# Two-layer retention and convolution trunk: early function table, longer warm-up, later rotary steps, one more staged weight unit

## The chip, the cores and the metric

The kernel runs on one core of one Trainium2 chip. The metric is the device time of one execution in microseconds (us). Before the change it is 840.92 us, the median of 3 runs (840.57 to 841.09).

## The reference, cut to what matters

```python
def reference(x, mem, positions, ...):          # x (1,512,1024), mem (1,256,1024), f32
    mem_k, mem_v = split(rmsnorm(mem, mem_norm_g) @ w_mem_kv)
    for i in range(2):
        h = rmsnorm(x, norm_pre_g[i])
        if i == 0: branch, xq, gate = retention_branch(h @ ret_w_in[0], positions)   # rotary q, k
        else:      branch, xq, gate = conv_branch(h @ conv_w_in[0], ...)             # 31 taps
        y = concatenate([branch, memory_attention(xq, mem_k, mem_v)]) * silu(gate)
        x = x + rmsnorm(y @ w_out, norm_post_g[i])
    return x
```

All is f32. The rotary embedding multiplies pairs of q and k by the cosine and sine of position times frequency.

## The kernel before, in words

Every engine runs its instructions in the order in which the program writes them; nothing is reordered afterwards. The program is written as projections of 16 chunks of matrix products, and `weave` puts other steps ("sides") behind a given chunk: `(5, x_rstd)` means that `x_rstd` is written behind chunk 5. A chunk's own loads and conversions are written when the chunk is, ahead of its products.

**Weights.** Each weight matrix is cut into units of 256 rows by 512 columns, used one after the other: units 0 to 7 for the memory's keys and values, 8 to 55 for the input projection of layer 0, 56 to 71 for its output projection, from 72 on for layer 1. Each product of f32 matrices is done as three products of rounded parts (`split3`, lines 302 to 304): high times high, high times low, low times high. So a unit is loaded by SP's queue into `wraw` (line 172, three buffers), cast by ScalarE to its high half `whi` (line 192), and the rest is computed as the low half `wlo`, on VectorE for some units (line 196), on POOL (GpSimd) for the others in two parts (line 199). There are five buffers each for the halves. `next_unit` hands out the halves of the next unit and converts some units ahead (`sent["ahead"]`: three in layer 0, one in the first projection of layer 1).

**Staged units.** For the units in `PRE` (even numbers, 76 to 110) the split is done during layer 0: `split_ahead` loads half a unit, casts it (line 228), subtracts on POOL (line 229) and stores both parts in a DRAM buffer `ahead` (line 219). One such step runs every 6 chunks (`ahead_hook`) from the second x projection on. When the unit is due, `conv_units` issues two loads on SP's queue instead (lines 182 and 183).

**The head.** ScalarE's queue loads `gcols` (norm weights, line 445) and `ident` (line 451). SP's queue loads `mem_t` in four parts, with units 0 to 2 between them. TensorE does 10 products of a block of ones with itself (line 461, two instructions each). ScalarE then scales `mem_t` to its high part (`split_c`, line 468), VectorE computes the low part (line 472). The projection of the memory's keys follows (16 chunks of 6 products of 256 columns, units 0 to 3, four chunks each), then that of its values.

**The first x projection** (`proj_halves`, 8 chunks of 12 products, units 8 to 11) gives values `v`. Its four results stay in their accumulators until the scale of the norm of x is known. `x_rstd` (behind chunk 5) sums the squares with small products (line 495), copies the sums on VectorE (line 497) and takes the power on POOL (lines 382 and 385); then ScalarE evacuates the four accumulators to `vb` (line 855). The next projection, xq (units 12 to 15), needs the same four accumulators. The diagonals of the scale (line 390) are built behind chunk 7.

**Rotary tables.** `rope_tables` is a generator of 25 steps: step 1 issues two DMAs of the positions, steps 2 to 21 are VectorE work on 128x256 tiles (range reduction), step 22 two sines on ScalarE (lines 825 and 826), the rest VectorE. `steps(n)` writes the next n of them.

**The start of layer 1.** The last phase of layer 0's output projection finishes token blocks 0 to 3 in turn; `post` updates a block with two VectorE instructions (line 732), `fin0` stores it to DRAM on SP's queue (line 1046), `sq` and `scale` (lines 1055 and 1060) norm it, and TensorE transposes it (line 406). Layer 1's first projection is `proj_halves` in its other form: chunks 0 to 15 do the first two token blocks with units 72 to 75, four chunks each, while blocks 2 and 3 are still on their way. Its sides are: 0 a transposition, 2 `post` of block 3 with its store, 4 the transposition of block 2, 5 and 7 the norm of block 3, 9 its transposition:

```python
weave(proj_halves(hT, evac_ug(0)), fill=0.95, sides=
      [(0, lambda: x1_T(3)), (2, post3), (4, x1_T2), (5, lambda: sq(3)), (7, lambda: scale(3)), (9, x1_T3)])
```

Unit 73 is converted in chunk 0, 74 in chunk 4 and 75 in chunk 8, 74 with its low half on POOL.

Of the kernel before, what the change touches and what calls it, by code (L numbers as in the profile page):

```python
# [13 lines left out]
AF = mybir.ActivationFunctionType  # L14
# [5 lines left out]
P = 128  # L20
# [16 lines left out]
GAMMA_LOG = np.log1p(-np.exp2(-5.0 - np.arange(NH, dtype=np.float64)))  # L37
CHUNK_DECAY = [float(np.exp(P * g)) for g in GAMMA_LOG]

WARM = 10  # L40
RATE = (1.6, 2.1, 1.9, 1.9, 1.7, 2.0, 1.7, 1.9, 2.1, 1.9)
XA = {0: (0, 7, 12), 1: (4, 13, 20), 2: (10, 17, 27), 3: (14, 22, 30)}
OFFLOAD = (0, 0.4, 0.8, 0.8, 0.8, 0.8, 0.8, 0.9, 0.8, 0.4, 0.5)
LN = (7, 32, 34, 36, 39)
LATE = 123
PRE = range(76, 112, 2)
MAGIC = 12582912.0
TWO_PI = 2.0 * math.pi

# [43 lines left out]
def trunk(ctx, tc, x, x_t, mem_t, pos, g_cols, w_mem, post_g, w0, w1, dw_w, dw_b,  # L93
          ln_g, ln_b, c_mask, c_xi, c_zeta, c_inv, c_eye, out):
    nc = tc.nc
# [9 lines left out]
    def nm(s):  # L105
        uid[0] += 1
        return f"{s}_{uid[0]}"

    def mm_ps():
        return ps.tile([P, 512], F32, tag="mm", bufs=4, name=nm("mm"))  # L110
# [7 lines left out]
    def big(dt, shape):  # L118
        return gp.tile(shape, dt, tag="big", bufs=8, name=nm("big"))
# [4 lines left out]
    def tiny(shape):  # L124
        return gp.tile(shape, F32, tag="tiny", bufs=32, name=nm("tiny"))
# [4 lines left out]
    nhalf = gp.tile([P, 8], F32, name="nhalf")  # L130
# [32 lines left out]
    def send(upto):  # L163

        for i in range(sent["dma"], min(upto, sent["conv"] + 3, nu)):
            sent["dma"] = i + 1
            if i in PRE:
                continue
# [5 lines left out]
    def conv_units(upto):  # L174
        for i in range(sent["conv"], min(upto, nu)):
# [4 lines left out]
            sent["conv"] = i + 1  # L180
            if i in PRE:
                nc.sync.dma_start(out=hi.bitcast(F32), in_=ahead[i][:, :, 1])
# [20 lines left out]

    ahead = {i: dp.tile([P, 2, 2, G], F32, name=f"ahead{i}") for i in PRE}

    def split_ahead(pool):

        todo = [(i, k) for i in PRE for k in range(2)]
        stage = {}

        def load(n):
            if n < len(todo):
                i, k = todo[n]
                stage[n] = pool.tile([P, 2, G], F32, tag="stage", bufs=3, name=nm("stage"))
                nc.sync.dma_start(out=stage[n][:, 0], in_=units[i][:, k * G:(k + 1) * G])

        def store(n):
            i, k = todo[n]
            nc.sync.dma_start(out=ahead[i][:, k], in_=stage.pop(n))

        load(0)
        yield
        for n in range(len(todo)):
            if n:
                store(n - 1)
            load(n + 1)
            st = stage[n]
            nc.scalar.copy(out=st[:, 1].bitcast(F32R), in_=st[:, 0])  # L228
            nc.gpsimd.tensor_tensor(out=st[:, 0], in0=st[:, 0], in1=st[:, 1], op=ALU.subtract)  # L229
            yield  # L230
        store(len(todo) - 1)
# [45 lines left out]
    def weave(chunks, sides=(), fill=0.0):  # L277
        phase[0] += bool(fill)
        at = {}
        for pos_, fn, *cost in sides:  # L280
            at.setdefault(pos_, []).append((fn, *cost, 0.0))
        due = more = 0.0
        for i, c in enumerate(chunks):
            c()
            due += fill
            for fn, cost, *_ in at.pop(i, ()):
                fn()
                due += fill * cost
            for hook in hooks:
                hook()  # L290
            while due >= 1 and (behind or filler and filler[0][2] in (None, *gls)):
                due -= filler[0][0] if filler else 1
                step()
            due = min(due, 2.0)
            more = min(more + OFFLOAD[phase[0]], 2.0) if fill else 0.0
            while more >= 1 and offload and offload[0]():
                more -= 1
        assert not at, at
# [7 lines left out]
    def proj(hT, tok_major, evac, n=S):  # L306

        cnt = n // P if tok_major else 4
        acc, unit = [], []

        def chunk(u, a):
            if not acc:
                acc.extend(mm_ps() for _ in range(cnt))
            if a == 0:
                unit[:] = next_unit()
            hi, lo = unit
            for k in range(2):
                kt = 2 * u + k
                hs = hT(kt)
                if tok_major:  # L320
                    lhs = tuple(t[:, a * P:(a + 1) * P] for t in hs)
                    split3(acc[a], lhs, (hi[:, k, :], lo[:, k, :]), kt == 0, kt == 7)
                else:
                    lhs = tuple(w[:, k, a * P:(a + 1) * P] for w in (hi, lo))
                    split3(acc[a][:, :n], lhs, hs, kt == 0, kt == 7)
            if u == 3:
                evac(a, acc[a])

        return [lambda u=u, a=a: chunk(u, a) for u in range(4) for a in range(cnt)]
# [112 lines left out]


    mt = big(F32, [P, KD, M])
    nc.scalar.dma_start(out=gcols, in_=g_cols.rearrange("p (a k) -> p a k", a=3))
    for c in range(4):
        nc.sync.dma_start(out=mt[:, 2 * c:2 * c + 2], in_=mem_t[:, c * G:(c + 1) * G]
# [11 lines left out]
    warm = mm_ps()  # L459
    for i in range(WARM):  # L460
        nc.tensor.matmul(warm[:, :P], ones, ones, start=True, stop=True)
# [3 lines left out]
    def split_c(src, kp, gcol, dst):  # L465

        for kt in (2 * kp, 2 * kp + 1):
            nc.scalar.activation(out=dst(kt)[0], in_=src[:, kt], func=AF.Copy,
                                 scale=gcol[:, kt:kt + 1])
        for kt in (2 * kp, 2 * kp + 1):  # L470
            hi, lo = dst(kt)
            nc.vector.scalar_tensor_tensor(out=lo, in0=src[:, kt], scalar=gcol[:, kt:kt + 1],
                                           in1=hi.bitcast(F32), op0=ALU.mult, op1=ALU.subtract)
# [3 lines left out]
    def squares(key, xt):  # L477

        sq = red[key] = [w4([P, KD // 2, 256]) for _ in range(2)]
        for i in range(2):  # L480
            nc.scalar.activation(out=sq[i], in_=xt[:, 4 * i:4 * i + 4], func=AF.Square)
        nc.gpsimd.tensor_tensor(out=sq[0], in0=sq[0], in1=sq[1], op=ALU.add)

    def reduced(key):
        sq = red[key]
        nc.vector.tensor_reduce(out=sq[1][:, 0], in_=sq[0].rearrange("p k s -> p s k"),
                                axis=AX.X, op=ALU.add)
        red[key] = sq[1][:, 0]
# [40 lines left out]
    xS = lambda half, kp: lambda: split_c(xp[half], kp, gcols[:, 1], hdst(half))  # L529
# [93 lines left out]
    def evac_copy(dst):  # L623
        return lambda a, acc: nc.scalar.copy(out=dst[:, a, :], in_=acc)
# [135 lines left out]
    with tc.tile_pool(name="l0", bufs=1) as lp:  # L760
# [84 lines left out]
        def steps(n):  # L845
            return lambda: [next(rope_steps, None) for _ in range(n)]
# [31 lines left out]
        def evac_gx(a, acc):  # L878
# [3 lines left out]
        sent["ahead"] = 3  # L882
        weave(proj_halves(hT, lambda t, acc: evac_vb(0)(t, acc) if "c" in rx else
                          late_v.append((t, acc)), True),
              [(0, steps(1))] + [(kp, xS(1, kp)) for kp in range(4)]
              + [(1, lambda: squares(1, xp[1])), (1, lambda: reduced(0)), (2, lambda: reduced(1)),
                 (5, x_rstd), (5, mem_diags), (7, x_diags)] + [(c, steps(2)) for c in range(4, 8)])
        pace["steps"] = split_ahead(lp)
        hooks.append(ahead_hook)
        weave(proj(hT, False, evac_copy(xq)), [(0, mem_spread), (1, x_spread)]  # L890
              + [(c, steps(2)) for c in range(16)])
        gx = big(F32, [P, XH, S])
        weave(proj(hT, False, evac_gx))
        yx = [big(F32R, [P, XH, S]) for _ in range(2)]
# [556 lines left out]
```

## Time and profile before

| | |
|---|---|
| median of 3 runs | 840.92 us (840.57 to 841.09) |
| the profiled execution | 841.23 us |
| its span, first to last instruction | 839.4 us |
| mean granted TensorE clock | 0.983 |
| TensorE busy | 805.0 us (96%) |
| VectorE busy | 507.5 us (60%) |
| ScalarE busy | 359.6 us (43%) |
| POOL busy | 437.0 us (52%) |

Times in the rows are us from the start of the span. PE is TensorE, DVE VectorE, ACT ScalarE, POOL GpSimd, SP the engine whose queue issues most DMAs; a q behind an engine's name is its queue. L302 is line 302. A busy TensorE is not TensorE at its peak, since its products overlap.

### The profile page before, as it was taken

What the parts mean: (1) busy time and instruction counts of PE and PEld (TensorE: products, weight loads), DVE (VectorE), ACT (ScalarE), POOL (GpSimd) and SP (SyncE); (2) the same over time, 40 slices, a digit from 0 to 9 for tenths busy, and PEclk for the clock granted to TensorE, in tenths of its full rate; (3) what the DMA queues carried; (4) which work ended last, traced back from release to release, by engine and by line L of the source; (5) the groups of instructions that cost most, each with busy time, mean ns of one, the idle gap of its engine ahead of it and who ended that gap; (6) DMA issues with size and microseconds to landing.
All of it is one profiled execution on the core that took longest, in us unless ns stands there. A gap on an engine that the chain in (4) does not pass through costs nothing.

```text
span 839.4 us, 10668 instructions
## 1 busy us (share of the span) xinstructions
PE 805.0 (96%) x3904; PEld 675.2 (80%) x3904; DVE 507.5 (60%) x794; ACT 359.6 (43%) x599; POOL 437.0 (52%) x390
## 2 busy tenths in 40 slices
PE   8999999999999999999999999999997995799997
PEld 8878888888888888888888988888876874388886
DVE  5898112143664641442437489999987999656423
ACT  6844366522212143433426234634676741166311
POOL 1145554467767766212233329969960993259202
PEclk9999999999999999999999999999998998799999
DMA  7623644364344445657743444444432212122712
GB/s 274 252 96 126 214 151 132 112 220 138 124 152 163 150 127 176 219 180 250 255 149 122 177 155 148 153 135 130 145 119 75 76 58 93 46 82 75 251 51 100
DMA packets 43171, 122.74 MB, mean 146 GB/s; under 512 B 4976, under 2 KB 6640, under 8 KB 42864
## 3 DMA queue, kind: packets, MB, share of 16 engines
q1 hardware_dynamic: 42688, 121.86, 42.6%
q8 instruction: 30, 0.49, 0.2%
q10 hardware_dynamic: 432, 0.21, 0.1%
q14 instruction: 21, 0.17, 0.1%
HBM read 98.99 MB, written 23.07 MB: 145 GB/s over the span
## 4 chain that ended last, share of the span: by engine, by line
PE 78%; DVE 15%; ACT 4%; issue 2%; POOL 1%; DMA 0%; POOLq 0%; DVEq 0%; ACTq 0%
PE mm L304 22%; PE mm L302 22%; PE mm L303 22%; DVE acc L1138 8%; DVE cy L1210 1%; PE tp L592 1%; PE acc L975 1%; PE tp L550 1%; PE tp L956 1%; PE acc L977 1%; PE acc L302 1%; PE acc L303 1%; PE acc L304 1%; PE tp L933 1%; ACT w L563 1%
## 5 line engine op out<-in xcount | busy, mean ns | idle before, releaser
L199 POOL TENSOR_TENSOR wlo<-wraw,whi 128x512 fp32r<-128x512 f32 x148 | 193.0, 1329 | 154.7 <-ACT whi L192 151.5
L302 PE MATMUL mm<-big,whi 128*128 128x512 f32 (+1 forms) x608 | 236.4, 389 | 4.6 <-ACT whi L188 1.9
L304 PE MATMUL mm<-big,wlo 128*128 128x512 f32 (+1 forms) x608 | 228.0, 375 | 0.2 <-DVE wlo L189 0.2
L303 PE MATMUL mm<-big,whi 128*128 128x512 f32 (+1 forms) x608 | 227.5, 374 | 0.0
L1138 DVE SCALAR_TENSOR_TENSOR acc<-gl,taps,acc 128x512 f32<-128x512 f32 x278 | 186.3, 748 | 0.4
L304 PE MATMUL mm<-whi,big 128*128 128x512 f32 (+1 forms) x432 | 166.9, 386 | 0.0
L302 PE MATMUL mm<-whi,big 128*128 128x512 f32 (+1 forms) x408 | 162.0, 397 | 0.0
L303 PE MATMUL mm<-wlo,big 128*128 128x512 f32 (+1 forms) x408 | 157.7, 387 | 0.2 <-DVE wlo L196 0.2
L192 ACT CAST whi<-wraw 128x1024 fp32r<-128x1024 f32 x115 | 119.3, 1047 | 39.5 <-PE mm L304 18.8
L302 PEld LDWEIGHTS mm<-big,whi 128*128 128x128 f32 x608 | 115.6, 190 | 24.9 <-ACT whi L188 2.2
L304 PEld LDWEIGHTS mm<-big,wlo 128*128 128x128 f32 x608 | 115.3, 190 | 21.3 <-DVE wlo L189 0.6
L303 PEld LDWEIGHTS mm<-big,whi 128*128 128x128 f32 x608 | 115.6, 190 | 19.3 <-issue 1.0
L229 POOL TENSOR_TENSOR stage<-stage 128x512 f32<-128x512 f32 x36 | 49.2, 1367 | 92.2 <-ACT stage L228 92.2
L1123 POOL TENSOR_TENSOR part<-part,pr 128x512 f32<-128x512 f32 x70 | 90.8, 1336 | 9.0 <-ACT pr L1122 9.0
L304 PEld LDWEIGHTS mm<-whi,big 128*128 128x128 f32 x432 | 81.1, 188 | 16.9
L303 PEld LDWEIGHTS mm<-wlo,big 128*128 128x128 f32 x408 | 76.8, 188 | 15.2 <-DVE wlo L196 0.7
L302 PEld LDWEIGHTS mm<-whi,big 128*128 128x128 f32 x408 | 76.7, 188 | 14.4
L196 DVE TENSOR_TENSOR wlo<-wraw,whi 128x1024 fp32r<-128x1024 f32 x41 | 56.4, 1388 | 43.4 <-ACT whi L192 43.3
L1122 ACT ACTIVATE pr<-gl,taps 128x512 f32<-128x512 f32 x70 | 47.6, 717 | 7.0 <-POOL part L1123 5.8
L228 ACT CAST stage<-stage 128x512 fp32r<-128x512 f32 x36 | 22.3, 620 | 48.3 <-DMA stage<-in_w 30.0
L948 ACT ACTIVATE kz<-tp,zeta 128x384 f32<-128x384 f32 x8 | 4.7, 584 | 78.1 <-PE tp L946 78.1
L1096 ACT ACTIVATE gl<-mm 128x512 f32<-128x512 f32 x12 | 7.2, 600 | 48.6 <-PE mm L304 48.6
(216 smaller groups left out, 895.5 us busy)
## 6 DMA issues: line engine op xcount, KB each, us to landing
wraw<-in_w SPq DMA_DIRECT2D x108, 512.0 KB, 4.1
ahead<-stage SPq DMA_DIRECT2D x36, 512.0 KB, 5.2
stage<-in_w SPq DMA_DIRECT2D x36, 256.0 KB, 5.2
whi<-ahead SPq DMA_DIRECT2D x18, 512.0 KB, 4.2
wlo<-ahead SPq DMA_DIRECT2D x18, 512.0 KB, 6.3
wraw<-in_w_mem SPq DMA_DIRECT2D x7, 512.0 KB, 4.8
big<-in_x_t SPq DMA_DIRECT2D x2, 1024.0 KB, 5.7
o<-in_x SPq DMA_DIRECT2D x1, 2048.0 KB, 9.0
```

The source lines that it names most:

```text
L192: nc.scalar.copy(out=hi, in_=raw)
L196: nc.vector.tensor_tensor(out=lo, in0=raw, in1=hi.bitcast(F32), op=ALU.subtract)
L199: nc.gpsimd.tensor_tensor(out=lo[:, k], in0=raw[:, k], in1=hi[:, k].bitcast(F32), op=ALU.subtract)
L228: nc.scalar.copy(out=st[:, 1].bitcast(F32R), in_=st[:, 0])
L229: nc.gpsimd.tensor_tensor(out=st[:, 0], in0=st[:, 0], in1=st[:, 1], op=ALU.subtract)
L302: nc.tensor.matmul(dst, lh, rh, start=start, stop=False)
L303: nc.tensor.matmul(dst, lh, rl, start=False, stop=False)
L304: nc.tensor.matmul(dst, ll, rh, start=False, stop=stop)
L550: nc.tensor.matmul(sc[:, j * M:(j + 1) * M], xq[:, h, t * P:(t + 1) * P], mkT[:, h, :], start=True, stop=True)
L1122: nc.scalar.activation(out=pr, in_=gl[:, k:k + S], func=AF.Copy, scale=tap)
L1123: nc.gpsimd.tensor_tensor(out=parts[ct], in0=parts[ct], in1=pr, op=ALU.add)
L1138: nc.vector.scalar_tensor_tensor(out=o, in0=gl[:, k:k + S], scalar=tap, in1=ac, op0=ALU.mult, op1=ALU.add)
```

## The change

Four edits. `WARM` goes from 10 to 13 products. `PRE` starts at 74 instead of 76, so that unit 74 is staged too (38 steps of half a unit instead of 36). A small activation on a constant (8 columns, filled by a memset at the start) is written ahead of the DMA of `gcols` on ScalarE's queue; the compiler puts the load of the function table ahead of the first activation. The rotary steps are written later: step 1 behind chunk 3 of the first x projection instead of chunk 0, two steps behind chunk 7 instead of two behind each of chunks 4 to 7, and then three behind each chunk of xq instead of two.

```diff
-WARM = 10
+WARM = 13
...
-PRE = range(76, 112, 2)
+PRE = range(74, 112, 2)
...
     mt = big(F32, [P, KD, M])
+    first = tiny([P, 8])
+    nc.scalar.activation(out=first, in_=nhalf, func=AF.Copy, scale=nhalf[:, 0:1])
     nc.scalar.dma_start(out=gcols, in_=g_cols.rearrange("p (a k) -> p a k", a=3))
...
-              [(0, steps(1))] + [(kp, xS(1, kp)) for kp in range(4)]
+              [(3, steps(1))] + [(kp, xS(1, kp)) for kp in range(4)]
               + [(1, lambda: squares(1, xp[1])), (1, lambda: reduced(0)), (2, lambda: reduced(1)),
-                 (5, x_rstd), (5, mem_diags), (7, x_diags)] + [(c, steps(2)) for c in range(4, 8)])
+                 (5, x_rstd), (5, mem_diags), (7, x_diags), (7, steps(2))])
...
         weave(proj(hT, False, evac_copy(xq)), [(0, mem_spread), (1, x_spread)]
-              + [(c, steps(2)) for c in range(16)])
+              + [(c, steps(3)) for c in range(16)])
```

## Rows read from the trace of the kernel before

**Rows 1.** The page: the chain that ended last, shares of the span by engine.

```profile
PE 78%; DVE 15%; ACT 4%; issue 2%; POOL 1%; DMA 0%; POOLq 0%; DVEq 0%; ACTq 0%
```

**Rows 2.** TensorE's waits, whole span: total us, times, longest us.

```profile
PE tp L406 <- DVE w L1060: 1.3, 1, 1.3
```

**Rows 3.** Timeline of ScalarE, head: start, us, what, count, idle before and its releaser.

```profile
4.75 1.28 ACT L468 ACT_TABLE_LOAD   x1 [4.75 <-DMA big<-in_mem_t]
6.04 0.91 ACT L468 ACTIVATE big<-big,gcols 128x256 fp32r<-128x256 f32 x2
...
11.53 0.91 ACT L468 ACTIVATE big<-big,gcols 128x256 fp32r<-128x256 f32 x2 [0.75 <-DMA big<-in_mem_t]
```

**Rows 4.** Timeline of TensorE, head: the warm-up.

```profile
1.01 4.63 PE L461 MATMUL mm<-ones 128*128 128x128 f32 x20 [1.01 <-POOL ones L140]
```

**Rows 5.** Windows, head: length, busy by engine, granted clock, DMA share, GB/s.

```profile
6.00:9.00 3.00, 1.27 (x6) 0.88 (x7) 2.40 (x5) 2.85 (x8) 0.00 (x0) 1.00 0.99 384
9.00:12.00 3.00, 3.00 (x17) 3.00 (x18) 2.56 (x5) 2.25 (x5) 0.00 (x0) 0.57 0.89 318
12.00:15.00 3.00, 3.00 (x24) 3.00 (x24) 2.50 (x5) 3.00 (x5) 0.00 (x0) 0.86 0.55 194
```

**Rows 6.** Waits of SP's queue, 0 to 7 us.

```profile
SPq L172 <- DMA gcols<-in_g_cols: 1.4, 1, 1.4
```

**Rows 7.** Timeline of VectorE, head: the low halves of units 2 and 3.

```profile
13.41 2.36 DVE L196 TENSOR_TENSOR wlo<-wraw,whi 128x1024 fp32r<-128x1024 f32 x2 [0.45 <-ACT whi L192]
```

**Rows 8.** Chain of waits, head: the first product of chunk 8 (start, us).

```profile
15.74 0.12 PE mm L302
```

**Rows 9.** Timeline of ScalarE: the first evacuation of the memory's values.

```profile
31.65 0.69 ACT L517 ACTIVATE mv<-mm,tiny 128x512 f32<-128x512 f32 x1 [0.82 <-PE mm L304]
```

**Rows 10.** Timeline of VectorE ahead of the norm's scale.

```profile
50.33 0.28 DVE L789 CAST q<-posi 128x256 f32<-128x256 int32 x1
...
54.72 0.15 DVE L497 COPY tiny<-tp 128x4 f32<-128x4 f32 x1
```

**Rows 11.** Timeline of POOL there.

```profile
50.92 2.59 POOL L199 TENSOR_TENSOR wlo<-wraw,whi 128x512 fp32r<-128x512 f32 x2 [6.22 <-ACT whi L192]
54.96 0.19 POOL L382 TENSOR_SCALAR tiny<-tiny 128x4 f32<-128x4 f32 x1 [1.45 <-DVE tiny L497]
55.24 1.25 POOL L385 TENSOR_TENSOR tiny<-tiny,nhalf 128x4 f32<-128x4 f32 x1
```

**Rows 12.** Timeline of TensorE there.

```profile
55.77 0.39 PE L304 MATMUL mm<-whi,big 128*128 128x512 f32 x1
57.26 0.50 PE L302 MATMUL mm<-big,whi 128*128 128x512 f32 x1 [1.11 <-ACT vb L855]
```

**Rows 13.** Timeline of ScalarE: the first evacuation of xq.

```profile
76.64 0.59 ACT L624 COPY big<-mm 128x512 f32<-128x512 f32 x1 [1.14 <-PE mm L304]
```

**Rows 14.** Timelines of VectorE and POOL at the start of layer 1.

```profile
431.43 0.75 DVE L732 SCALAR_TENSOR_TENSOR o<-o,tiny 128x512 f32<-128x512 f32 x1 [0.38 <-POOL tiny L377]
...
451.29 1.61 DVE L732 SCALAR_TENSOR_TENSOR o<-o,tiny 128x512 f32<-128x512 f32 x1
452.83 1.77 DVE L732 SCALAR_TENSOR_TENSOR o<-ra,tiny,o 128x512 f32<-128x512 f32 x1
...
451.08 2.97 POOL L199 TENSOR_TENSOR wlo<-wraw,whi 128x512 fp32r<-128x512 f32 x2 [2.29 <-ACT whi L192]
```

**Rows 15.** Timeline of SP's queue there: the store of the last token block.

```profile
454.63 0.32 SPq L1046 DMA_DIRECT2D x1d<-o  x1
```

**Rows 16.** Issue to landing of the 18 loads of line 182, then of 183.

```profile
DMA to landing us min/median/max: 4.1/4.2/7.7
...
DMA to landing us min/median/max: 4.9/6.3/8.4
```

**Rows 17.** Timeline of TensorE, layer 1: unit 74's first low product, and chunk 10.

```profile
454.59 0.28 PE L304 MATMUL mm<-big,wlo 128*128 128x256 f32 x1
...
458.12 0.37 PE L302 MATMUL mm<-big,whi 128*128 128x256 f32 x1
```

## The prediction

> **What bounds the kernel now.** I read the chain of waits first: TensorE holds 78% of it and VectorE 15% [rows 1], and the VectorE part lies late in layer 1. So up to there a microsecond counts only if TensorE stands still in it or runs at the lower clock. Then I read TensorE's waits, its timeline around each wait, and last the engine that was waited for. Three places matter here.
>
> At the head, the products at line 461 end at 5.64 and the first real product starts at 7.5. In 6 to 9 us TensorE is busy 1.27 of 3.00, and the granted clock then stands at 0.57 and 0.86 in the next two stretches [rows 4, 5]: together (0.43 + 0.14) × 3 / 0.5 = 3.4 us at 1.2 instead of 2.4 GHz.
>
> At 55 us, the last product of the first x projection starts at 55.77 and the next one only at 57.26; at a step of 0.23 us, 1.26 us are lost. It waits for the first evacuation of `vb`, that one for POOL's power at 55.24 to 56.49, and that for VectorE's copy at 54.72 [rows 10 to 12]. Ahead of the copy VectorE ran rotary steps from 50.33 on.
>
> At the start of layer 1, TensorE waits 1.3 us at line 406 for the scale of the last token block [rows 2].
>
> **The function table.** The load takes 1.28 us and starts when the first quarter of `mem_t` has landed; the first activation follows at 6.04 [rows 3]. With the load done early, that activation waits for its data alone: mem_t by 4.7, and `gcols`, which landed at about 4.9 (a load of the third weight unit waited 1.4 us for just that landing [rows 6], since loads share completion counters). Now `gcols` is issued behind the table load and the small activation. How far that delays it the trace doesn't show, since no DMA stands behind a table load in it. Bounds: 0.1 us, if the queue passes the DMA on while the engine still loads; 1.28 + 0.46, if it holds it (half of the pair at 6.04, 0.91 us, is more than 8 columns can take [rows 3]). I take 0.1, as nothing in the DMA needs the engine. The first activation then starts at about 5.1 instead of 6.04; at the other end at about 6.7, and the third unit's load may then slip by the same 1.7 us.
>
> The Trainium skill ("Perfetto Trace Analysis", section "DVE / Act Engine Instruction") says that the sequencer is free again once it has pushed an activation into the wait queue, so the DMA would not wait for the load. By it the activation starts at 5.1, by a holding queue at 6.7; both give the same end below within 0.8 us.
>
> For what follows is set by data: the fourth quarter of mem_t lands at 11.53, ScalarE stands for it 0.75 us [rows 3], and only then casts units 2 and 3. So unit 2's low half stays ready at 14.6 (13.41 + half of 2.36 [rows 7]) however early the table is. TensorE used it first in the third product of chunk 8, 15.74 + 0.24 = 15.98 [rows 8]. So there are 1.4 us to gain at most, and TensorE can take them, because unit 1 is ready earlier still and three more warm products (six instructions of 4.63/20 = 0.23 us [rows 4]) run to about 7.0 and leave almost no idle time ahead of the first real one. Even a second fall of the clock would only use up time before 14.6. Further on, ScalarE caps it: it idles 0.82 us before the evacuation at 31.65 [rows 9], and its casts of units 10 and 11 stand behind that. Value **0.8 us gained**; bounds 0 and 1.4.
>
> **Rotary tables behind the scale.** Steps 2 to 9 leave the four chunks before the norm's scale; two come after the diagonals, the rest three a chunk. VectorE has unit 13's low half (1.2 us) left ahead of its copy, POOL unit 14's low halves, 2.59 us from 50.92 to 53.51 [rows 11]. So POOL is what comes last: it starts the scale at 53.55 instead of 54.96, and the first evacuation ends 1.4 us earlier, at about 55.8 against TensorE's 56.0. **1.26 us gained**, the whole gap, bounds 0 and 1.3; it holds if TensorE is 0.8 earlier, since POOL's unit 14 waits for TensorE to free a buffer. The positions' two DMAs move from chunk 0 to chunk 3, past no other load on SP's queue. The moved VectorE work, about 4 us, ends later: the two sines and the casts behind them come about 1 us later while TensorE is 2 us earlier. ScalarE has 1.14 us idle ahead of the next evacuation [rows 13] and the four accumulators are needed again only from 3.2 us later, so it costs nothing; were the tables over 3 us later, the excess would be lost.
>
> **One more staged unit.** Unit 74 is the third of layer 1's first projection, used from chunk 8 on. Its split moves into layer 0 (two more casts, two more subtractions, four more DMAs, in the last two paces of 6 chunks before the layer's end; they lie beside products, and the first scales needed there have over 2 us of slack): nothing. In layer 1 its cast and its two POOL subtractions go. Those, 2.97 us from 451.08, lie over VectorE's two updates of the last token block, which took 1.61 and 1.77 [rows 14]; without them I take 0.75 each, what the first of block 0 took [rows 14], and the scale comes 1.7 us earlier. That alone would remove the whole 1.3 us wait.
>
> But its halves now come by two loads on SP's queue, and they are issued in chunk 4, behind the store of the last token block (side 2), which waits for these very updates. The store went out at 454.63 [rows 15]; it now goes at about 452.85. Behind it the high half goes at 453.25 and the low half at 453.95 (issues of 0.32 and about 0.7). Landings of 18 such loads: 4.1 to 7.7 us for the high half, 4.9 to 8.4 for the low one, medians 4.2 and 6.3 [rows 16]. So the high half is there at 457.4, the low one between 458.8 and 462.3; I take 459.8, under the median sum of 460.2 because the queues are empty then. TensorE wants the low half at 454.59 [rows 17] (all in the time of before; the 2 us gained shift both sides alike).
>
> From that product to chunk 10 are 4 products and one chunk of 6 at 0.12 us a product [rows 8], and 8 transposes, 0.85 us: 0.48 + 0.72 + 0.85 = 2.05. Chunk 10 started at 458.12, wait included [rows 17]; now at 459.8 + 2.05 = 461.9. **3.8 us lost**, bounds 2.7 and 6.2. TensorE also does next to nothing from 454.4 to 459.8, less than in the stretch before the clock fell at the head [rows 5]. I expect the same fall: 3.4 us at half speed, **1.7 us lost**; bounds 0 and 3.4.
>
> The Trainium skill ("SBUF — State Buffer", section "SBUF: two separate sides") says that VectorE and GpSimd hold a shared port pair for whole instructions. The stretched updates agree (1.61 against 0.75), and by this rule alone the third edit is a gain of 1.3 us, which is the first rival.
>
> **The sum** on the profiled execution, 841.23 us (span 839.4 and 1.8 around it): − 0.8 − 1.26 + 3.8 + 1.7 = + 3.4, so 844.7; that execution lies 0.3 above the median of 840.92, so **844.4 us**. Layer 1 passes a delay on, because its VectorE work starts with the first projection's result.
>
> **Rivals.**
> - *The staged unit is in time*: its halves land before 454.6, TensorE loses its 1.3 us wait instead, and the time is 840.92 − 2.1 − 1.3 = 837.5. For it: the stretched updates are real, and other staged units are waited for nowhere. Against: those are issued far ahead, this one four chunks ahead. It needs issues at least 6 us ahead of use, that is ahead of the store. The change ends faster than before if the low half is used before about 458.1 and the clock stays up: 3.5 us over the 454.59.
> - *The stall without the fall of the clock*: 842.7. For it: a wait of 1.3 us here left no mark; against, the stall is four times as long.
> - *The head doesn't do what it says* (the DMA of gcols held, the third unit late, or the gap at 56 filled by something else): + 0.8 to + 2.1 on the forecast, 845.2 to 846.5.
> - *The edits at the head do what they say and more*: up to 1.4 there, 843.8; inside the range.
>
> **How the numbers follow.** Forecast 0.53, stall without the clock 0.15, unit in time 0.14, head without gain 0.13, else 0.05. What differs by under 0.2% (1.7 us) can't be told from no change. Faster by more than that: the unit in time, and a little else, 0.16. Within: half of the second rival and the forecast's low end (both halves landing at their fastest), 0.15. Slower: 0.69. The range leaves out the unit in time (0.14) and little above: 840.5 to 847.0; the forecast's own is 842.5 to 846.
>
> **What would show it.** Head: table load before 2.2 us, first activation near 5.1, no clock under 1.00 before 13 us or none that costs. At 55 us: the copy at line 497 some 4 us earlier against its neighbours, no wait of line 302 for `vb`. Layer 1: the updates at line 732 at 0.75 each, no wait of line 406, and in its place a TensorE wait of 4 to 6 us at line 302 and 304 for DMA of `whi` and `wlo` from `ahead`, with a clock near 0.5 behind it. Without that last wait the prediction is wrong.

## The result and the profile after

The changed kernel takes 846.05 us (median of 6 runs, 845.09 to 847.79), the kernel before 840.95 us beside it (6 runs, 839.74 to 841.47). The ratio is 1.0066 (95% interval 1.0053 to 1.0079), so 4.5 to 6.6 us slower. The profiled execution took 845.96 us, its span is 844.2.

The chain that ended last, from the page, and TensorE's waits of the whole span (total us, times, longest us). These answer to [rows 1, 2].

```profile
PE 76%; DVE 14%; ACT 4%; DMA 3%; issue 1%; POOL 1%; SPq 0%; POOLq 0%; DVEq 0%; ACTq 0%
```

```profile
PE mm L302 <- DMA whi<-ahead: 4.1, 1, 4.1
PE mm L303 <- DVE wlo L196: 1.9, 1, 1.9
PE mm L304 <- DMA wlo<-ahead: 0.6, 1, 0.6
```

DMA has come into the chain with 3%; it had 0%. The waits of 1.3 us at line 406 and of 1.1 us for `vb` are gone, and in their place stand 4.1 and 0.6 us for the two halves of a staged unit, and 1.9 us for a low half that VectorE makes.

I set the start of each TensorE instruction against that of the same instruction before (after minus before, us). The line numbers are 2 higher behind line 445.

```
at        25    41    50    57   451   472   632   639   718   724   span
change  -0.9  +0.9  +0.9  -0.4  -0.4  +5.4  +5.4  +4.5  +5.1  +4.2  +4.8
```

Three places hold most of it: 1.8 us lost between 25 and 41, 1.3 won at 57, 5.8 lost at 454 to 466.

**Head.** ScalarE's timeline, then three stretches (busy us of TensorE, its weight loads, VectorE, ScalarE and POOL; granted clock, DMA share, GB/s), as [rows 3, 5].

```profile
0.72 1.28 ACT L446 ACT_TABLE_LOAD   x1 [0.72 <-PEq L1444]
0.86 0.39 ACTq L447 DMA_DIRECT2D gcols<-in_g_cols  x1
...
5.02 0.91 ACT L470 ACTIVATE big<-big,gcols 128x256 fp32r<-128x256 f32 x2 [2.71 <-DMA gcols<-in_g_cols]
```

```profile
6.00:9.00 3.00, 2.78 (x20) 2.32 (x19) 2.53 (x6) 2.56 (x5) 0.00 (x0) 1.00 1.04 415
9.00:12.00 3.00, 2.88 (x24) 2.68 (x23) 2.53 (x5) 2.26 (x6) 0.00 (x0) 1.00 0.87 337
12.00:15.00 3.00, 2.73 (x23) 2.53 (x22) 2.55 (x3) 3.00 (x4) 0.00 (x0) 1.00 0.35 135
```

The table load runs from 0.72, `gcols` is issued at 0.86, inside it, and the first activation starts at 5.02. The clock doesn't fall.

**The scale of the norm.** VectorE's copy and the first evacuation of `vb`, as [rows 10, 12].

```profile
52.15 0.15 DVE L499 COPY tiny<-tp 128x4 f32<-128x4 f32 x1
```

```profile
56.07 2.42 ACT L857 ACTIVATE vb<-mm,tiny 128x512 f32<-128x512 f32 x4 [4.31 <-POOL tiny L385]
```

**Start of layer 1.** SP's queue, VectorE's two updates, TensorE's products of unit 74, and the stretches there, as [rows 14, 15, 17].

```profile
452.35 0.32 SPq L1048 DMA_DIRECT2D x1d<-o  x1
452.76 0.59 SPq L182 DMA_DIRECT2D whi<-ahead  x1
453.40 0.62 SPq L183 DMA_DIRECT2D wlo<-ahead  x1
```

```profile
450.92 0.74 DVE L734 SCALAR_TENSOR_TENSOR o<-o,tiny 128x512 f32<-128x512 f32 x1
451.58 0.75 DVE L734 SCALAR_TENSOR_TENSOR o<-ra,tiny,o 128x512 f32<-128x512 f32 x1
```

```profile
458.26 0.58 PE L302 MATMUL mm<-big,whi 128*128 128x256 f32 x1 [4.11 <-DMA whi<-ahead]
...
459.60 0.58 PE L304 MATMUL mm<-big,wlo 128*128 128x256 f32 x1 [0.55 <-DMA wlo<-ahead]
```

```profile
454.00:457.00 3.00, 0.15 (x2) 0.00 (x0) 1.89 (x2) 0.01 (x1) 0.28 (x3) 0.95 0.91 234
457.00:460.00 3.00, 1.19 (x4) 0.90 (x5) 0.00 (x0) 0.00 (x0) 0.00 (x0) 0.50 1.02 399
460.00:463.00 3.00, 3.00 (x16) 3.00 (x16) 0.00 (x0) 0.43 (x2) 0.00 (x0) 0.50 1.03 388
463.00:466.00 3.00, 3.00 (x25) 3.00 (x24) 2.56 (x7) 2.60 (x8) 0.00 (x0) 0.91 0.26 101
```

The updates take 0.75 each, so the store goes at 452.35. The loads of unit 74 go behind it, at 452.76 and 453.40. TensorE's last product ahead of them starts at 453.87; the high half is there at 458.26, the low one at 459.60. Then the products run 0.21 us apart instead of 0.12, for the clock stands at 0.50, 1.2 instead of 2.4 GHz, until past 463.

### The profile page after: what moved, and what is told of

It is laid out like the page before. It is cut to its first block, busy times and chain, and to the rows that moved or that the text cites. A ratio compares the mean times of both kernels' runs of the same rounds, so it can differ in the third digit from the quotient of the medians.

```text
span 844.2 us, 10690 instructions
## 1 busy us (share of the span) xinstructions
PE 806.0 (95%) x3910; PEld 676.2 (80%) x3910; DVE 509.3 (60%) x794; ACT 360.0 (43%) x601; POOL 436.2 (52%) x390
## 4 chain that ended last, share of the span: by engine, by line
PE 76%; DVE 14%; ACT 4%; DMA 3%; issue 1%; POOL 1%; SPq 0%; POOLq 0%; DVEq 0%; ACTq 0%
PE mm L304 21%; PE mm L302 21%; PE mm L303 21%; DVE acc L1140 9%; DVE cy L1212 1%; PE tp L594 1%; PE acc L977 1%; DMA big<-in_mem_t 1%; DMA wraw<-in_w_mem 1%; PE tp L958 1%; PE acc L979 1%; PE acc L302 1%; PE acc L303 1%; PE acc L304 1%; PE tp L935 1%
## 5 line engine op out<-in xcount | busy, mean ns | idle before, releaser
L199 POOL TENSOR_TENSOR wlo<-wraw,whi 128x512 fp32r<-128x512 f32 x146 | 190.4, 1329 | 160.4 <-ACT whi L192 142.0
L229 POOL TENSOR_TENSOR stage<-stage 128x512 f32<-128x512 f32 x38 | 52.0, 1369 | 88.5 <-ACT stage L228 88.5
L302 PEld LDWEIGHTS mm<-whi,big 128*128 128x128 f32 x408 | 76.7, 188 | 14.5
```

Of the source, the lines that this page charges most:

```text
L199: nc.gpsimd.tensor_tensor(out=lo[:, k], in0=raw[:, k], in1=hi[:, k].bitcast(F32), op=ALU.subtract)
L302: nc.tensor.matmul(dst, lh, rh, start=start, stop=False)
```

## The experiments

Each time is a median, with its ratio to the kernel before, measured beside it (840.95 to 841.38 in the comparisons below), and the interval of the ratio. A ratio's distance from 1, times 841, gives the us that I compare.

### The parts one at a time

The kernel before with `PRE = range(74, 112, 2)` alone:

> The kernel before with the staging of unit 74 alone. Theory A (the late loads of unit 74 are the whole loss): TensorE waits 4 to 6 us for whi and wlo at the start of layer 1, runs behind it at half clock, stands 5 to 6 us later than before from 470 us on, and keeps 4.5 to 5.5 us of it at the end: 845.4 to 846.4. Rival B (the stall is worth less, and part of the loss comes from the edits at the head): under 843.5. Rival C (the unit in time): 839.6.

With the small activation and `WARM = 13` alone:

> The kernel before with the early table load and 13 warm products alone. Theory A (the loads of the weights end last in the first 50 us): 0.9 us ahead at 25 us, all of it lost again in a wait for a later weight unit by 50 us, since its load lands no earlier; time within 0.6 us of before, 840.3 to 841.5. Theory of the prediction (ScalarE's 0.8 us of idle time is the only cap, the gain stays): 840.1. Rival (the edit itself makes loads land later): 841.5 to 843.

With the rotary steps moved alone:

> The kernel before with the rotary steps moved alone. Theory of the prediction: the wait of 1.1 us for the first evacuation of vb at 57 us goes, nothing comes late behind it, 839.7. Rival (the gap closes only because TensorE came 0.9 us later to it in the changed kernel, or another engine is last there): 840.4 to 841.

The changed kernel with `PRE = range(76, 112, 2)`:

> The changed kernel with unit 74 taken out of the staged ones again. By the prediction's sum: 840.92 - 0.8 - 1.26 = 838.9. Theory A with the head's gain lost again in the wait for a weight unit near 40 us: 840.92 - 0.45 = 840.5. The difference from the changed kernel is the price of the staged unit: 5.1 to 7 us.

```
                     us      ratio   interval         against before
staged unit alone    848.32  1.0077  1.0063 - 1.0090   +6.5
head alone           841.79  1.0004  0.9995 - 1.0013   +0.3
rotary steps alone   840.11  0.9987  0.9979 - 0.9996   -1.1
all but staged       840.99  0.9997  0.9987 - 1.0006   -0.3
changed kernel       846.05  1.0066  1.0053 - 1.0079   +5.6
```

The parts add up: 6.5 + 0.3 - 1.1 = 5.7 against 5.6. The staged unit is the whole loss (theory A; its expected 845.4 to 846.4 was too low), the rotary steps do what they should, and the head gives nothing, where 840.1 was forecast.

### What the staged unit waits for

The store of the last token block is put behind unit 74's loads:

```diff
 def fin0(t, y):
     ...
-    nc.sync.dma_start(out=x1d[t * P:(t + 1) * P, :], in_=y)
+    if t < 3:
+        nc.sync.dma_start(out=x1d[t * P:(t + 1) * P, :], in_=y)
     nxt["y", t] = y
+def store3():
+    nc.sync.dma_start(out=x1d[3 * P:4 * P, :], in_=nxt["y", 3])
 ...
-      [(0, lambda: x1_T(3)), (2, post3), (4, x1_T2), ...
+      [(0, lambda: x1_T(3)), (2, post3), (4, store3), (4, x1_T2), ...
```

> The changed kernel with the store of the last token block issued behind the loads of unit 74 in place of ahead of them. Theory A (the loads are late because they stand behind that store on SP's queue): issued up to 6 us earlier, halves there by 454, no wait for whi or wlo and no fall of the clock, and the wait of 1.3 us at line 406 doesn't come back: 841.0 - 1.3 = 839.7. Rival B (the loads wait for their buffers or for the staged data, not for the store): 845 to 846.5, as the changed kernel. Rival C (the wait moves to unit 76 or to the scale of the block): 841 to 843.

839.35 us, ratio 0.9974 (0.9963 to 0.9985). SP's queue (line 1053 is the store in its new place), and TensorE's stretches:

```profile
446.59 0.76 SPq L182 DMA_DIRECT2D whi<-ahead  x1
447.40 1.23 SPq L183 DMA_DIRECT2D wlo<-ahead  x1
...
453.38 0.33 SPq L1053 DMA_DIRECT2D x1d<-o  x1
```

```profile
454.00:457.00 3.00, 3.00 (x27) 3.00 (x27) 1.79 (x2) 1.17 (x4) 0.94 (x4) 1.00 0.93 294
457.00:460.00 3.00, 3.00 (x28) 3.00 (x27) 2.35 (x7) 2.90 (x8) 0.00 (x0) 1.00 0.94 331
```

The loads go 6 us earlier, TensorE waits for nothing between 440 and 475, and its clock stays at 1.00. Neither the buffers nor the staged data held them: the store did. Ahead of the store the staged unit is the gain that it was meant to be, since line 406 doesn't wait either: 1.9 us less than all but staged by the ratios.

To part the wait from the clock, 40 transposes are put into it:

```diff
+def again():
+    for _ in range(5):
+        for kp in range(4):
+            transp(late["pt"][kp], [nxt[2], None], kp, (0,))
 ...
-      (7, lambda: scale(3)), (9, x1_T3)])
+      (7, lambda: scale(3)), (7, again), (9, x1_T3)])
```

> The changed kernel with 40 transposes of 0.11 us more in front of chunk 8 of layer 1's first projection, where TensorE waits for unit 74: the eight transposes of the third token block, five times over into the same place. They fit into the wait of 4.1 us but for some 0.3 us. Theory A (the wait costs 3.8 to 4.1 us and the clock that falls in it 1.7 more): the clock stays at 1.00, and the end comes 1 to 1.7 us earlier, 844.4 to 845.1. Rival (the fall of the clock costs nothing, or the wait lasts only as long as TensorE is idle): 846 to 850.

845.12 us, 1.0043 (1.0030 to 1.0057), so 1.9 us less than the changed kernel by the ratios. The same stretch in its windows and the first low product:

```profile
457.00:460.00 3.00, 3.00 (x30) 3.00 (x27) 0.51 (x1) 0.00 (x0) 0.00 (x0) 1.00 0.94 304
460.00:463.00 3.00, 2.28 (x20) 2.07 (x19) 0.00 (x0) 0.36 (x1) 0.00 (x0) 1.00 1.02 376
```

```profile
460.93 0.38 PE L304 MATMUL mm<-big,wlo 128*128 128x256 f32 x1 [0.72 <-DMA wlo<-ahead]
```

TensorE uses the low half as late behind the store as before (453.79 to 460.93, 7.1 us; in the changed kernel 452.35 to 459.60, 7.2), so the low half doesn't land sooner. The clock stays up, and across this stretch TensorE goes from 1.45 us behind the changed kernel to 0.47 ahead. So the fall costs 1.9 of the 5.8 us, and the wait, less the 1.3 us that line 406 no longer waits, 3.9. Only this stretch of the trace is compared: its execution, 847.09, is the slowest of the five, and had already lost 1.5 us at 42 to 46, where its clock fell to half. The medians say 1.9 as well, but their intervals overlap, from 1.0053 to 1.0057.

### Where the head's gain goes

The transposed x, `x_t`, is loaded in two halves of 1 MB. Its second half is put behind unit 12, first without the staged unit, and then on the kernel with the store behind:

```diff
-   (4, xS(0, 1)), (4, lambda: x_load(1)), (5, conv(10)), (5, xS(0, 2)),
+   (4, xS(0, 1)), (5, conv(10)), (5, lambda: x_load(1)), (5, xS(0, 2)),
```

> The changed kernel without the staged unit 74, and with the load of the second half of x_t (1 MB) issued behind that of unit 12 in place of ahead of it. Theory A (the product at 40 to 41 us waits for unit 12, which lands behind that megabyte whatever the head does, and this ate the head's 0.8 us): unit 12 is cast before 39, the wait of 2 us at line 303 is under 0.5, TensorE is 1.5 us or more ahead of the run without this edit at 41 us; if the x half is in time for its use at 48 us, 839.0 to 839.7; if it is late there, 840.5 to 842. Rival (the loads before unit 12 are the pace, this order changes nothing): 840.6 to 841.4 with the wait unchanged.

> Store behind the loads of unit 74, and x_t's second half behind unit 12, on the changed kernel with all its parts. Theory A: both gains add, 838.0 to 838.8, which beats both kernels. Rivals: as the store alone (839.7), if the x half is late; over 840.9, if neither wait goes.

841.20 us (1.0001, 0.9991 to 1.0012) and 839.76 (0.9980, 0.9970 to 0.9990): nothing won over the kernels without the edit. ScalarE and TensorE of the first:

```profile
37.67 1.99 ACT L192 CAST whi<-wraw 128x1024 fp32r<-128x1024 f32 x2
```

```profile
41.37 0.50 PE L303 MATMUL mm<-wlo,big 128*128 128x512 f32 x1 [2.11 <-DVE wlo L196]
```

Units 11 and 12 are cast by 39.66 (37.67 + 1.99), unit 12 some 2 us earlier than in the changed kernel, and TensorE waits as long. My theory fell: the product at 41 wants the low half of unit 11. The rows of the changed kernel, ScalarE, VectorE and TensorE:

```profile
34.91 0.68 ACT L519 ACTIVATE mv<-mm,tiny 128x512 f32<-128x512 f32 x1
35.49 2.00 ACT L483 ACTIVATE w<-big 128x1024 f32<-128x1024 f32 x2
37.38 1.04 ACT L192 CAST whi<-wraw 128x1024 fp32r<-128x1024 f32 x1
```

```profile
38.46 2.57 DVE L196 TENSOR_TENSOR wlo<-wraw,whi 128x1024 fp32r<-128x1024 f32 x1 [2.19 <-ACT whi L192]
```

```profile
41.08 0.50 PE L303 MATMUL mm<-wlo,big 128*128 128x512 f32 x1 [1.93 <-DVE wlo L196]
```

`mv` holds the memory's values. From its second evacuation (34.91) ScalarE does the squares of x and the cast of unit 11, and VectorE its low half, beside POOL's sum of the squares. In twelve traces with this order the product starts 6.16 to 6.21 us after that evacuation, whatever the head does; where it starts:

```
without the head's edits (4 traces)   40.17  40.94  41.05  41.17
with them (5)                         40.43  40.49  40.60  41.00  41.08
wait ahead of it                      0.2 to 0.8 without, 1.5 to 2.1 with
```

The five are those with the loads in the changed kernel's order; the other three with the head's edits start it at 40.48, 41.17 and 41.37, behind waits of 1.0 to 2.1. So the head brings TensorE earlier to 25 us, and it waits longer at 41. The trace of the kernel before (40.17) is the earliest of the four, so up to 1.0 of the 1.8 us lost between 25 and 41 may belong to that execution and not to the change. No run moved the start of the chain, the evacuation at 34 to 35, by itself.

Next I took this chain apart. Squares behind the cast of unit 11, on the kernel with the store behind:

```diff
-   (6, xS(0, 3)), (6, conv(11)), (7, lambda: squares(0, xp[0]))])
+   (6, xS(0, 3)), (6, conv(11))])
 ...
-   [(3, steps(1))] + [(kp, xS(1, kp)) for kp in range(4)]
+   [(3, steps(1)), (0, lambda: squares(0, xp[0]))] + [(kp, xS(1, kp)) for kp in range(4)]
```

> The kernel with the store behind (839.35), and the squares of the first x half behind the cast of unit 11 in place of ahead of it. In eight traces the product at 40 to 41 starts 6.2 us after ScalarE's evacuation of mv that precedes the squares: 0.6 evacuation, 2.0 squares, 1.0 cast, 2.6 for VectorE's low half of unit 11 beside POOL's sum of those squares (1.2 without it). Theory A (this chain, not a load, ate the head's gain): the low half is ready 3 us earlier, the wait of 2.0 us goes, and the squares, now later, must not hold the second x half (used at 48 us): 838.0 to 838.4 if they don't, 839.0 to 839.6 if the wait moves there. Rival (the load of unit 12 is the pace): 839.4 with a wait of 1.5 to 2 us for unit 12 at the next four products.

The small load of `ln_b` taken from ahead of unit 7's load and put behind x_t's second half, so that unit 7's takes another completion counter (in the changed kernel it waited 2.2 us for the landing of x_t's first half, which the same semaphore counts); and both edits:

> The kernel with the store behind (839.35), with one small constant's load taken from the six behind the first x half and put behind the second, so that the load of unit 7 no longer shares its completion counter with the first x half (1 MB, landing at 20.5 to 23 us) and needn't wait for it. Theory B (that landing sets the loads of units 7 to 10, these set ScalarE's order of casts, and so the evacuation of mv ahead of the squares): unit 7's load goes at 19.7 to 20.6 in place of 22.3, the wait at 40 us shrinks by 1 us or more, 838.2 to 838.6. Rival (transfers share a full set of engines, so an earlier issue lands no earlier): 839.0 to 839.8, with unit 7's cast within 0.5 us of 25.6.

> Both edits on the kernel with the store behind. Theory A and B each right: as the better of the two, 837.6 to 838.4, with the head's 0.8 us kept at 48 us. If the second x half or the norm's scale at 56 us comes last instead: 838.8 to 839.6.

841.17 (0.9991, 0.9981 to 1.0002), 839.38 (0.9972, 0.9960 to 0.9984) and 840.07 (0.9985, 0.9974 to 0.9996). VectorE and TensorE of the first:

```profile
38.42 1.22 DVE L196 TENSOR_TENSOR wlo<-wraw,whi 128x1024 fp32r<-128x1024 f32 x1 [2.03 <-ACT whi L192]
```

```profile
39.70 0.50 PE L303 MATMUL mm<-wlo,big 128*128 128x512 f32 x1 [0.53 <-DVE wlo L196]
...
46.83 0.80 PE L304 MATMUL mm<-whi,big 128*128 128x512 f32 x1 [1.59 <-DVE big L474]
```

The wait for unit 11 shrinks from 2.0 to 0.5, and the same subtraction takes 1.22 instead of 2.57. But the second x half, now behind the squares, is late, with 0.6 and 1.6 us of waits at 44.5 and 46.8 and a clock of 0.79 and 0.64 in the two stretches from 45 to 51; the kernel is 1.4 us slower than with the store behind alone by the ratios, though their intervals overlap a little. In the second one, SP's queue and ScalarE:

```profile
20.71 0.38 SPq L172 DMA_DIRECT2D wraw<-in_w_mem  x1
```

```profile
26.32 1.05 ACT L192 CAST whi<-wraw 128x1024 fp32r<-128x1024 f32 x1 [0.83 <-DMA wraw<-in_w_mem]
```

Unit 7's load goes at 20.71 instead of the 22.32 of the kernel with the store behind, and is cast at 26.32 instead of 25.61: an earlier issue landed no earlier, as the rival had it. The wait for x_t's first half moved to the next load, unit 8's, which waits 2.0 us. The wait at 41 is 1.0 here, but because TensorE comes to it 0.9 us later: the product starts at 40.48, against 40.60. The time can't be told from 839.35; theory B's 838.2 to 838.6 lies inside its interval too, so one trace speaks against it, not the time. With both edits the wait at 41 is gone, and one of 1.0 us for the x half stands at 44.8. So behind the first 25 us stand several bounds within about 1 us of each other (the loads, ScalarE's order, the x halves). Which of them is worth moving first these runs don't settle.

Last, the kernel with the store behind without the head's edits (no small activation, `WARM = 10`):

> The kernel with the store behind (839.35) without the head's edits: the table load and the 10 warm products as in the kernel before, the rotary steps moved, unit 74 staged. Theory A (a later bound in the first 50 us takes the head's gain and no more, so its edits are worth nothing): 839.0 to 839.7. Theory C (they cost 0.4 to 0.9, as the difference of head alone to before and of rotary and head to rotary alone has it): 838.3 to 838.9. By the prediction's 0.8 of gain: 840.1.

838.78 us, 0.9970 (0.9959 to 0.9980): the fastest median here, 2.5 us under the kernel before by its ratio. That is what theory C expected, but against 839.35 with the head's edits the intervals overlap, so whether these cost something isn't shown; a gain of 0.8 lies outside the interval of the head alone (0.4 at most). A way in which they can cost is seen in TensorE's stretches of the kernel with the store behind:

```profile
39.00:42.00 3.00, 1.40 (x4) 1.16 (x5) 2.60 (x2) 2.13 (x4) 0.46 (x1) 0.83 0.33 124
42.00:45.00 3.00, 3.00 (x9) 2.33 (x9) 3.00 (x6) 3.00 (x6) 0.51 (x1) 0.60 0.83 289
```

Its wait of 2.0 us at 40.6 is followed by a clock of 0.60, and between 41 and 60 us it loses 1.6 us to the trace of all but staged, which waited 2.1 at the same place and kept 1.00. Of ten traces with the head's edits three show such a fall between 39 and 51 us (one of them behind the waits at 44.5 and 46.8), of four without none.

## Why the prediction was right, and where it was off

Forecast 844.4 in 840.5 to 847.0, measured 846.05: slower, by the mechanism named, and just above the 842.5 to 846 that the prediction gave its forecast alone. The 1.65 us between them are by the medians mostly one term.

- *Function table: the step held, its gain did not.* The activation starts at 5.02 (forecast 5.1), and the queue passes the DMA on 0.15 us later (0.86 instead of 0.71), inside the table load (0.72 to 2.00). The rule that the prediction took from the Trainium skill ("Perfetto Trace Analysis", section "DVE / Act Engine Instruction") agrees with this row. The low product of chunk 8 starts at 14.11, 1.7 earlier than in the timeline before (15.81), more than the 1.4 given as the most: the fourth quarter of `mem_t` had landed by 10.95 instead of 11.53. In the trace of the head alone it came at 11.58 again, and the product at 14.76, 1.1 earlier. The failing step is "ScalarE caps it: it idles 0.82 us before the evacuation at 31.65, and its casts of units 10 and 11 stand behind that". The cap was taken as the gain. But in the changed kernel ScalarE waits for the loads behind its casts at 24.09 and 26.18 (2.2 and 1.1 us; 1.5 and 0.9 before) and has no idle time left ahead of that evacuation, and unit 11's low half is there at 40.4 to 41.1, where it is at 40.2 to 41.2 without the head's edits. Sized 0.8 gained, measured 0.3 lost (0.4 gained to 1.1 lost): 1.1 of the 1.65.
- *Rotary tables: right.* 1.26 forecast, 1.1 measured alone (0.3 to 1.8), 1.3 in the trace. The proviso that TensorE must be 0.8 earlier was not met: in every trace with this part TensorE comes 0.3 us or more later to 55 than in the kernel before, and the gap closes even so. The rival that it closes only because TensorE is late falls by the traces: in the three without this part TensorE waits 0.7 to 1.1 us for `vb`, 0.8 in the staged unit alone, where it comes 1.0 later; in the eleven with it 0 to 0.2. Nothing came late behind it.
- *Staged unit: right, place and size.* Updates 0.75 each as forecast; store, high half, low half in this order. The low half was used 6.2 us after its issue (median 6.3; the 459.8 taken meant 5.9), the wait cost 3.9 (3.8 forecast), the clock 1.9 (1.7 forecast); against all but staged the whole is 5.8 us by the ratios (5.5 forecast). "I expect the same fall" was the weaker half of the argument, from one case at the head; it held in both kernels that have the wait and not in the one whose wait was filled.
- *That alone would remove the whole 1.3 us wait*: shown by the store behind, where line 406 doesn't wait. The updates of 1.61 and 1.77 beside POOL became 0.75 each, and a subtraction of 2.57 beside POOL's sum became 1.22 without it. The rule that the prediction took from the Trainium skill ("SBUF — State Buffer", section "SBUF: two separate sides") agrees with both.
- *Layer 1 passes a delay on*: nearly. Of 5.4 us 1.2 were given back from 632 to 724. In the staged unit alone, 6.1 us there became 6.9. So this differs by execution, and nothing shows it to be the change's doing.
- *Rivals.* The unit in time fell as described, and its condition, issues at least 6 us ahead of use and ahead of the store, is what the store behind met. The stall without the clock is the kernel with work in the wait. The head without gain had 0.13, and its 845.2 to 846.5 holds the 846.05; but of its reasons none came about (`gcols` wasn't held, the third unit wasn't late, the gap at 56 closed). The gain was lost in a place that the prediction didn't look at.

## What to carry to other kernels

A transfer that replaces work is as early as its place in its queue: read what stands ahead of it there, and what that waits for, before counting the work that it saves. A gain at the head of a kernel lasts to the next place where TensorE nearly waits; follow the chain of that place (here 6.2 us over ScalarE and VectorE) before booking it. A stall of TensorE is priced with the clock behind it, and work put into the wait parts the two.

## What the runs showed of the hardware

The first half of x_t (1 MB) landed 5.4, 5.4, 6.9 and 7.1 us after its issue in the four traces without the head's edits, which run the same instructions up to there. So the same transfer differs by 1.7 us from one execution to another, more than the terms argued over at the head: a single trace of this stretch can't carry 0.8 us. In the ten traces with the head's edits it took 6.9 to 8.3 us. It was issued at 14.5 to 15.6 there and at 15.0 to 15.7 without them, and landed at 21.8 to 23.1 against 20.4 to 22.6, so an earlier issue landed no earlier. After a wait of 1.9 to 2.1 us at 41 the clock stood at 0.58 and 0.60 from 42 to 45 in two traces and stayed at 1.00 in four. After the wait of 4 us at 454 it was 0.50 from 460 to 463 in the changed kernel and 0.59 in the staged unit alone.
